# Triangular blocks of the DeltaNet inversion: substitution in blocks of sixteen, two per partition, merged to thirty-two on TensorE

## The chip, the core and the metric

The kernel runs on one core of a Trainium2 chip. The metric is the device time of one execution in microseconds (us); where several executions are timed, their median counts.

## What is computed

A trunk of two layers on a sequence of 1024 positions of width 1024. Each layer projects the normalised input once, gives the columns to three mixers (a convolution module, differential attention, and a gated DeltaNet in both directions), joins them in an output projection and ends in an MLP:

```python
u = rms_norm(x, pre_mix_w[l]) @ w_in[l]
y = concat([conv_module(u_conv, ...), diff_attention(dq, dk, dv, ...), gated_deltanet(gqkv, gz, ...)]) @ w_out[l]
x = x + rms_norm(y, post_mix_w[l])
x = x + rms_norm(square(relu(rms_norm(x, pre_mlp_w[l]) @ w_ff1[l])) @ w_ff2[l], post_mlp_w[l])
```

The change concerns the DeltaNet. It works in chunks of 64 positions, and each chunk, head (6) and direction (2) needs the solution with a unit lower triangular 64x64 matrix:

```python
A = where(strict, einsum("bhncd,bhnsd->bhncs", kb, kc) * decay, 0.0)
sol = triangular_solve(A, rhs, left_side=True, lower=True, unit_diagonal=True)
```

The scan over the 16 chunks (`step` in the reference) uses that solution, chunk after chunk.

## The kernel before

`w_in_phase` computes the input projection as dense items of 48 matmuls of 512 columns (L163 to L165, three products of high and low parts), in the order of the list `todo`: convolution inputs and DeltaNet q, k, v (`cp_0` to `cp_8`), attention q and k (`qkh`), attention v (`vt`), and the gate z (`zt`). Between the items two generators are advanced: `conv_module`, and `prep`, which makes for each of three head pairs p the masked products A (`dn_a`: transposes L652, squares `sq` on ACT L654, products of k and q L696, `R` and `De` on GpSimd L682 and L686, the powers `rkinv` and `rq` L670), and then runs `invert` for that pair beside `dn_a` of the next. The last five items of `todo` stand behind the end of `prep`; the DeltaNet scan (`scan`, first matmul L837) and its loads (`qkT`, `eg`, `vs`, `kta`) are advanced beside them.

`invert` (L736 to L804) turns the 64x64 triangles into their inverses. It writes A to DRAM (`ai`, L750) and reads it back so that each of the 128 partitions holds one diagonal block of 32x32 (`Lr`, `Lp`, L754); ACT transposes half of them (L755). On GpSimd, 31 rounds of two operations follow, each round a product with a column of `Lp` (L765, tile `subt`) and a subtraction in `Xm` (L766), on up to 256 elements per partition. ACT writes the transpose `XT` (L768). Both go to DRAM (`xi`, L770 and L771), and twelve loads bring them back as `Ta` and into the diagonal blocks of `Tt` (L779, L782). On TensorE, 64 products with `Ao` (the off-diagonal block of A) and 64 products with `Tt` give the off-diagonal block (L789 and L790, L797 and L798, tile Y between them on ACT); the inverse `Tt` is written to `kta` (L804). This runs six times, three pairs in two layers.

Every engine works through its own instructions in a fixed order, which a scheduler sets when the kernel is built: it lays the instructions out by a time plan of its own, so an edit in one function also moves instructions of others. Waits are by semaphores: an instruction that waits holds all that stands behind it on its engine. SP (SyncE) issues most of the DMAs, one after the other, in its order.

Of the kernel before, what the change touches and what calls it, by code (L numbers as in the profile page):

```python
# [9 lines left out]
F32 = mybir.dt.float32  # L10
F32R = mybir.dt.float32r
BF16 = mybir.dt.bfloat16
AF = mybir.ActivationFunctionType
ALU = mybir.AluOpType
# [4 lines left out]
P = 128  # L19
# [10 lines left out]
CH = 64  # L30
# [7 lines left out]
def make_consts():  # L38
    p = np.arange(P)
    t, s = p[:, None], p[None, :]  # L40
    same = (t // CH) == (s // CH)
    c64 = np.arange(CH)[None, :]
    pm = (p % CH)[:, None]
    cols, off = [], {}

    def add(name, a):
        a = np.asarray(a, np.float32)
        off[name] = (sum(c.shape[1] for c in cols), a.shape[1])
        cols.append(a)

    add("ident", np.eye(P))
    add("gt0", same & (t > s))
    add("gt1", same & (t < s))
    add("cum0", same & (t <= s))
    add("cum1", same & (t >= s))
    add("n0", np.where(pm <= c64, 30000.0, -30000.0))
    add("n1", np.where(pm >= c64, 30000.0, -30000.0))
    qs = np.zeros((P, 3))
    for j in range(3):
        for h in range(2):  # L60
            qs[64 * h:64 * h + 64, j] = -np.float32(DD ** -0.5) * 2.0 ** SLOPE_EXP[2 * j + h]
    add("qs", qs)
    return np.concatenate(cols, 1), off


CONSTS, COFF = make_consts()
BIAS = np.abs(np.arange(P)[:, None] - (np.arange(1920)[None, :] - 896)).astype(np.float16)

# [10 lines left out]
class K:  # L79
# [656 lines left out]
    def invert(self, l, p, A, X):  # L736

        nc = self.nc
        mm = nc.tensor.matmul
        nm = f"{l}_{p}"  # L740
        B = 32
        Lr = X.tile([P, B, B], F32, tag="Lr", bufs=2, name=f"Lr{nm}")
        Lp = X.tile([P, B, B], F32, tag="Lp", bufs=2, name=f"Lp{nm}")
        Af = [t.rearrange("p m h c -> p (m h) c") for t in A]
        Ao = X.tile([P, 16, B], F32, tag="Ao", bufs=1, name=f"Ao{nm}")
        for g in range(4):
            r = slice(g * B, (g + 1) * B)
            nc.sync.dma_start(Ao[r], Af[g % 2][r, :, B - (g % 2) * B:2 * B - (g % 2) * B])
        for d in range(2):
            nc.sync.dma_start(self.ai[p % 2][d], A[d].rearrange("p m h c -> p (m h c)"))  # L750
            dst = Lp if d else Lr
            for g in range(4):
                src = self.ai[p % 2][d, g * B:(g + 1) * B, :].rearrange("r (m c) -> m r c", c=CH)[:, :, (g % 2) * B:(g % 2 + 1) * B]
                nc.sync.dma_start(dst[64 * d + 16 * g:64 * d + 16 * g + 16], src)  # L754
        nc.scalar.activation(Lp[0:64], Lr[0:64].rearrange("p a b -> p b a"), AF.Copy)  # L755
        yield
        Xm = X.tile([P, B, B], F32, tag="Xm", bufs=1, name=f"Xm{nm}")
        XT = X.tile([P, B, B], F32, tag="Lr", bufs=2, name=f"XT{nm}")
        nc.gpsimd.memset(Xm, 0.0)
        nc.gpsimd.memset(Xm.rearrange("p a b -> p (a b)")[:, ::B + 1], 1.0)  # L760
        for j in range(B - 1):
            n, w = B - 1 - j, j + 1
            tmp = X.tile([P, 256], F32, tag="subt", bufs=1, name=f"subt{nm}_{j}")
            tv = tmp[:, 0:n * w].rearrange("p (a b) -> p a b", b=w)
            nc.gpsimd.tensor_tensor(tv, Lp[:, j + 1:, j:j + 1].broadcast_to([P, n, w]), Xm[:, j:j + 1, 0:w].broadcast_to([P, n, w]), op=ALU.mult)  # L765
            nc.gpsimd.tensor_tensor(Xm[:, j + 1:, 0:w], Xm[:, j + 1:, 0:w], tv, op=ALU.subtract)  # L766
            yield
        nc.scalar.activation(XT, Xm.rearrange("p a b -> p b a"), AF.Copy)  # L768
        xi = self.xi[p % 2]
        nc.sync.dma_start(xi[0], Xm)  # L770
        nc.sync.dma_start(xi[1], XT)  # L771
        Tt = [X.tile([P, NT, 2, CH], F32, tag=f"Tt{d}", bufs=1, name=f"Tt{nm}_{d}") for d in range(2)]
        for d in range(2):
            nc.gpsimd.memset(Tt[d], 0.0)
        Ta = X.tile([P, 16, B], F32, tag="iv", bufs=2, name=f"Ta{nm}")
        for g in range(4):
            r = slice(g * B, (g + 1) * B)
            for d in range(2):
                nc.sync.dma_start(Tt[d].rearrange("p m h c -> p (m h) c")[r, :, (g % 2) * B:(g % 2 + 1) * B],  # L779
                                  xi[1 - d, 64 * d + 16 * g:64 * d + 16 * g + 16].rearrange("m r c -> r m c"))  # L780
            d = g % 2
            nc.sync.dma_start(Ta[r], xi[d, 64 * d + 16 * g:64 * d + 16 * g + 16].rearrange("m r c -> r m c"))  # L782
        yield
        ps = self.dt_bank().rearrange("p (g c) -> p g c", c=B)
        Tf = [t.rearrange("p m h c -> p (m h) c") for t in Tt]
        for g in range(16):
            for hf in range(2):
                lo, hi = slice(64 * hf, 64 * hf + B), slice(64 * hf + B, 64 * hf + 2 * B)
                mm(ps[hi, g], lhsT=Ao[lo, g], rhs=Ta[lo, g], start=True, stop=True, tile_position=(64 * hf, 64 * hf + B))  # L789
                mm(ps[lo, g], lhsT=Ao[hi, g], rhs=Ta[hi, g], start=True, stop=True, tile_position=(64 * hf + B, 64 * hf))  # L790
        Y = X.tile([P, 16, B], F32, tag="iv", bufs=2, name=f"Y{nm}")
        nc.scalar.activation(Y, ps, AF.Copy, scale=-1.0)
        ps = self.dt_bank().rearrange("p (g c) -> p g c", c=B)
        for g in range(16):
            for hf in range(2):
                lo, hi = slice(64 * hf, 64 * hf + B), slice(64 * hf + B, 64 * hf + 2 * B)
                mm(ps[lo, g], lhsT=Y[hi, g], rhs=Tf[0][hi, g, B:], start=True, stop=True, tile_position=(64 * hf + B, 64 * hf))  # L797
                mm(ps[hi, g], lhsT=Y[lo, g], rhs=Tf[1][lo, g, :B], start=True, stop=True, tile_position=(64 * hf, 64 * hf + B))  # L798
        for hf in range(2):
            lo, hi = slice(64 * hf, 64 * hf + B), slice(64 * hf + B, 64 * hf + 2 * B)  # L800
            nc.scalar.activation(Tf[0][lo, :, B:], ps[lo], AF.Copy)
            nc.vector.tensor_copy(Tf[1][hi, :, :B], ps[hi])
        for d in range(2):
            nc.sync.dma_start(self.kta[d, :, :, 1, p].rearrange("m q c -> q m c"), Tt[d].rearrange("p m h c -> p m (h c)"))  # L804
# [800 lines left out]
```

## Time and profile before

| | before |
|---|---|
| runs | 2982.74, 2984.09, 2980.22 us, median 2982.74 |
| profiled execution | 2982.14 us, of it span 2980.3 us |
| mean granted TensorE clock | 0.955 |
| PE (TensorE) busy | 2726.6 us, 91% |
| DVE (VectorE) busy | 2093.7 us, 70% |
| ACT (ScalarE) busy | 1391.1 us, 47% |
| POOL (GpSimd) busy | 892.1 us, 30% |
| chain that ended last | PE 65%, POOL 11%, DVE 8%, DMA 8% |

Busy time says how long an engine had work in progress; the chain that ended last follows the work back from the last instruction, at each step to what it waited for. The clock column of the windows is the share of full speed (2.4 GHz; the lower level is 1.2 GHz, shown as 0.5) that was granted. A number in brackets behind a row of the timeline is the time that the engine stood idle before it, and what released it.

### The profile page before, as it was taken

Reading aid. Unit: us, or ns where it says so; the run is one execution under the profiler, and the core shown is the slowest. Engines: PE = TensorE matmul, PEld = TensorE weight load, DVE = VectorE, ACT = ScalarE, POOL = GpSimd, SP = SyncE. Lnnn points to the kernel's source line nnn. Section 1 sums busy time; section 2 is a strip of 40 time slices with the busy share of each in tenths; the row PEclk is TensorE's granted clock in tenths of the full one; section 3 lists DMA queues with packets and bytes.
Section 4 is the critical chain, followed back from the end, with each engine's and each line's share of the span. In section 5 each row is a group of like instructions: output and inputs, shape, how many; then the busy total and the mean of one; then the engine's idle time right before and its main releaser. Section 6 shows DMA issues by size and latency. Waiting matters only on the chain.

```text
span 2980.3 us, 46140 instructions
## 1 busy us (share of the span) xinstructions
PE 2726.6 (91%) x17292; PEld 2184.5 (73%) x17292; DVE 2093.7 (70%) x3717; ACT 1391.1 (47%) x2436; POOL 892.1 (30%) x801
## 2 busy tenths in 40 slices
PE   8977979988999998999799689799989999989996
PEld 7865757766888886888687567577668888878885
DVE  5796327888487776777757772279874877767776
ACT  5432326676256664333354223266863566643232
POOL 2288716756000000000313986267541000000002
PEclk9998979999999999999899889799989999999998
DMA  5557785433235558664446486844332355586643
GB/s 136 152 153 210 207 201 154 120 102 124 81 110 212 200 196 315 224 213 165 130 121 140 130 244 188 213 133 124 101 120 85 114 211 201 216 335 223 215 142 113
DMA packets 415313, 504.74 MB, mean 169 GB/s; under 512 B 125401, under 2 KB 313945, under 8 KB 412786
## 3 DMA queue, kind: packets, MB, share of 16 engines
q1 hardware_dynamic: 359362, 373.92, 42.0%
q10 hardware_dynamic: 55728, 127.88, 11.2%
q8 instruction: 136, 2.23, 0.3%
q14 instruction: 87, 0.71, 0.1%
HBM read 318.01 MB, written 182.12 MB: 168 GB/s over the span
## 4 chain that ended last, share of the span: by engine, by line
PE 65%; POOL 11%; DVE 8%; DMA 8%; issue 4%; ACT 2%; SPq 2%; ACTq 0%; DVEq 0%; POOLq 0%
PE at L163 10%; PE at L164 10%; PE at L165 10%; POOL Xm L766 4%; PE sc L163 4%; PE sc L164 4%; PE sc L165 4%; POOL subt L765 3%; PE at L1044 2%; PE dt L163 2%; PE dt L165 2%; PE dt L164 2%; PE tr L1070 2%; DVE sc L1046 2%; PE tr L1079 2%
## 5 line engine op out<-in xcount | busy, mean ns | idle before, releaser
L246 POOL TENSOR_TENSOR y<-y,mgP 128x1024 f32<-128x1024 f32 x8 | 21.8, 2737 | 1247.5 <-ACT jk L242 1247.5
L163 PE MATMUL at<-hTh,wh 128*128 128x512 f32 (+1 forms) x832 | 328.1, 396 | 7.7 <-ACT cp L363 7.7
L165 PE MATMUL at<-hTh,wl 128*128 128x512 f32 (+1 forms) x832 | 326.7, 394 | 6.9 <-DVE wl L169 6.9
L164 PE MATMUL at<-hTl,wh 128*128 128x512 f32 (+1 forms) x832 | 327.5, 394 | 0.0
L1049 ACT ACTIVATE sc<-sc,mx 128x1024 f32<-128x1024 f32 x192 | 220.8, 1152 | 88.8 <-DVE mx L1046 88.6
L163 PEld LDWEIGHTS at<-hTh,wh 128*128 128x128 f32 x832 | 161.3, 194 | 39.6 <-ACT cp L363 8.5
L165 PEld LDWEIGHTS at<-hTh,wl 128*128 128x128 f32 x832 | 160.9, 194 | 39.5 <-DVE wl L169 8.4
L164 PEld LDWEIGHTS at<-hTl,wh 128*128 128x128 f32 x832 | 161.6, 194 | 31.2 <-issue 0.8
L491 DVE SCALAR_TENSOR_TENSOR ca<-cu,dw,ca 128x1024 f32<-128x1024 f32 x120 | 170.6, 1437 | 0.4
L1044 PE MATMUL at<-stk 96*128 96x512 f32 x352 | 144.9, 470 | 16.1 <-DVE mx L1046 14.9
L1046 DVE CUSTOM_DVE_ANT_0 sc<-at,bias,mx 128x512 f32<-128x512 f32 x192 | 142.3, 745 | 21.8 <-PE at L1044 16.3
L1046 DVE CUSTOM_DVE_ANT_0 sc<-at,bias 128x512 f32<-128x512 f32 x192 | 130.0, 684 | 35.4 <-PE at L1044 32.1
L1156 ACT ACTIVATE ob<-sb 128x512 fp32r<-128x512 f32 x120 | 74.2, 626 | 171.8 <-PE tr L165 45.4
L765 POOL TENSOR_TENSOR subt<-Lp,Xm 128x31 f32<-128x31 f32 (+15 forms) x186 | 129.5, 696 | 82.9 <-DMA Lp<-ai 25.8
L766 POOL TENSOR_TENSOR Xm<-Xm,subt 128x31 f32<-128x31 f32 (+15 forms) x186 | 144.3, 776 | 13.0
L163 PE MATMUL at<-ob,oa 128*128 128x512 f32 x356 | 138.5, 391 | 1.0 <-DVE y L1482 1.0
L164 PE MATMUL at<-ob,oa 128*128 128x512 f32 x356 | 139.0, 391 | 0.0
L165 PE MATMUL at<-ob,oa 128*128 128x512 f32 x356 | 138.9, 390 | 0.0
L1156 ACT ACTIVATE ob<-w2r 128x512 fp32r<-128x512 f32 x92 | 57.3, 627 | 141.7 <-PE tr L165 52.2
L1070 PE MATMUL tr<-consts,sc 128*128 128x128 f32 x704 | 108.0, 284 | 12.9 <-DVE sc L1066 6.0
L169 DVE TENSOR_TENSOR wl<-wr,wh 128x1024 fp32r<-128x1024 f32 x48 | 65.1, 1356 | 72.4 <-ACT wh L168 72.4
L1157 DVE TENSOR_TENSOR ob<-sb,ob 128x512 fp32r<-128x512 f32 x120 | 81.6, 686 | 41.3 <-ACT ob L1156 41.3
(459 smaller groups left out, 7950.7 us busy)
## 6 DMA issues: line engine op xcount, KB each, us to landing
hd<-oa ACTq DMA_DIRECT2D x120, 512.0 KB, 5.8
oa<-hd SPq DMA_DIRECT2D x120, 512.0 KB, 4.3
w1r<-in_w_ff_dram SPq DMA_DIRECT2D x32, 1024.0 KB, 5.6
w2r<-in_w_ff_dram SPq DMA_DIRECT2D x64, 512.0 KB, 6.5
wr<-in_w_in_dram SPq DMA_DIRECT2D x50, 512.0 KB, 5.2
ld<-hd SPq DMA_DIRECT2D x98, 256.0 KB, 3.9
kta<-kta SPq DMA_DIRECT2D x32, 576.0 KB, 9.4
stk<-qk SPq DMA_DIRECT2D x66, 256.0 KB, 6.2
```

The costliest lines, as they stand in the source:

```text
L163: mm(ps, lhsT=lh, rhs=rh, start=first, stop=False, skip_group_check=more)
L164: mm(ps, lhsT=lh, rhs=rl, start=False, stop=False, skip_group_check=more)
L165: mm(ps, lhsT=ll, rhs=rh, start=False, stop=last, skip_group_check=more)
L491: nc.vector.scalar_tensor_tensor(ca, u[:, k:k + S], dw[:, i, k:k + 1], ca, ALU.mult, ALU.add)
L765: nc.gpsimd.tensor_tensor(tv, Lp[:, j + 1:, j:j + 1].broadcast_to([P, n, w]), Xm[:, j:j + 1, 0:w].broadcast_to([P, n, w]), op=ALU.mult)
L766: nc.gpsimd.tensor_tensor(Xm[:, j + 1:, 0:w], Xm[:, j + 1:, 0:w], tv, op=ALU.subtract)
L1044: mm(ps, lhsT=st[:, 0, t * P:(t + 1) * P], rhs=st[:, 1, ks], start=True, stop=True)
L1046: nc.vector.tensor_tensor_reduce(out=sc[:, ks], in0=ps, in1=self.bias[:, o:o + 512], scale=slope, scalar=mx[:, 0:1] if n2 else 3.0e38, op0 ...
L1049: nc.scalar.activation(sc, sc, AF.Exp, scale=-1.0, bias=mx[:, 1:2], accum_out=oS[:, t, mp:mp + 1])
L1070: nc.tensor.transpose(ps[:, k], pp[0][:, (4 * q + k) * P:(4 * q + k + 1) * P], self.ident)
L1156: self.nc.scalar.activation(h, src, AF.Copy)
L1157: self.nc.vector.tensor_tensor(lo, src, h.bitcast(F32), op=ALU.subtract)
```

## The change

Substitution is done in blocks of sixteen. Each partition still holds its 32x32 block, but GpSimd works on the two 16x16 blocks of the diagonal at once: 15 rounds of two operations on up to 128 elements. `Lp` has one buffer instead of two, `subt` two instead of one. What joins the two halves of a block of 32 is new: tiles `Oz` (two per inversion) hold the off-diagonal 16x16 blocks, set to zero by GpSimd and filled by ACT with row masks `rm0` and `rm1`; a tile `Tb` holds the other orientation of the inverse; sixteen loads of `xi` take the place of twelve. TensorE then makes 128 products of 32 columns with `Oz` (ACT copies the result back into `Oz`), 64 for `Ta`, and 128 of 64 columns for `Tt`, and VectorE subtracts the results from `Ta` and `Tt`. The step to 64 is as before. All 32x32 work of TensorE keeps its four diagonal positions.

```diff
@@ -60,6 +60,8 @@
         for h in range(2):
             qs[64 * h:64 * h + 64, j] = -np.float32(DD ** -0.5) * 2.0 ** SLOPE_EXP[2 * j + h]
     add("qs", qs)
+    add("rm0", (p % 32 < 16)[:, None])
+    add("rm1", (p % 32 >= 16)[:, None])
     return np.concatenate(cols, 1), off
 
 
@@ -738,9 +740,18 @@
         nc = self.nc
         mm = nc.tensor.matmul
         nm = f"{l}_{p}"
-        B = 32
-        Lr = X.tile([P, B, B], F32, tag="Lr", bufs=2, name=f"Lr{nm}")
-        Lp = X.tile([P, B, B], F32, tag="Lp", bufs=2, name=f"Lp{nm}")
+        B, H = 32, 16
+        W = H * B + H
+
+        def blocks(t):
+
+            return t.rearrange("p (x k) -> p x k", k=W)[:, :, 0:H * B].rearrange("p x (a b) -> p x a b", b=B)
+
+        def square(t):
+            return t[:, 0:B * B].rearrange("p (a b) -> p a b", b=B)
+
+        Lr = X.tile([P, 2 * W], F32, tag="Lr", bufs=2, name=f"Lr{nm}")
+        Lp = X.tile([P, 2 * W], F32, tag="Lp", bufs=1, name=f"Lp{nm}")
         Af = [t.rearrange("p m h c -> p (m h) c") for t in A]
         Ao = X.tile([P, 16, B], F32, tag="Ao", bufs=1, name=f"Ao{nm}")
         for g in range(4):
@@ -748,41 +759,80 @@
             nc.sync.dma_start(Ao[r], Af[g % 2][r, :, B - (g % 2) * B:2 * B - (g % 2) * B])
         for d in range(2):
             nc.sync.dma_start(self.ai[p % 2][d], A[d].rearrange("p m h c -> p (m h c)"))
-            dst = Lp if d else Lr
+            dst = square(Lp if d else Lr)
             for g in range(4):
                 src = self.ai[p % 2][d, g * B:(g + 1) * B, :].rearrange("r (m c) -> m r c", c=CH)[:, :, (g % 2) * B:(g % 2 + 1) * B]
                 nc.sync.dma_start(dst[64 * d + 16 * g:64 * d + 16 * g + 16], src)
-        nc.scalar.activation(Lp[0:64], Lr[0:64].rearrange("p a b -> p b a"), AF.Copy)
+
+        Oz = [X.tile([P, 16, B], F32, tag="Oz", bufs=2, name=f"Oz{nm}_{d}") for d in range(2)]
+        for d in range(2):
+            nc.gpsimd.memset(Oz[d], 0.0)
+            o = H - H * d
+            for g in range(4):
+                r = slice(g * B, (g + 1) * B)
+                nc.scalar.activation(Oz[d][r, :, o:o + H], Af[d][r, :, (g % 2) * B + o:(g % 2) * B + o + H], AF.Copy, scale=self.C[f"rm{d}"][r])
+        nc.scalar.activation(square(Lp)[0:64], square(Lr)[0:64].rearrange("p a b -> p b a"), AF.Copy)
         yield
-        Xm = X.tile([P, B, B], F32, tag="Xm", bufs=1, name=f"Xm{nm}")
-        XT = X.tile([P, B, B], F32, tag="Lr", bufs=2, name=f"XT{nm}")
+        Xm = X.tile([P, 2 * W], F32, tag="Xm", bufs=1, name=f"Xm{nm}")
+        XT = X.tile([P, 2 * W], F32, tag="Lr", bufs=2, name=f"XT{nm}")
         nc.gpsimd.memset(Xm, 0.0)
-        nc.gpsimd.memset(Xm.rearrange("p a b -> p (a b)")[:, ::B + 1], 1.0)
-        for j in range(B - 1):
-            n, w = B - 1 - j, j + 1
-            tmp = X.tile([P, 256], F32, tag="subt", bufs=1, name=f"subt{nm}_{j}")
-            tv = tmp[:, 0:n * w].rearrange("p (a b) -> p a b", b=w)
-            nc.gpsimd.tensor_tensor(tv, Lp[:, j + 1:, j:j + 1].broadcast_to([P, n, w]), Xm[:, j:j + 1, 0:w].broadcast_to([P, n, w]), op=ALU.mult)
-            nc.gpsimd.tensor_tensor(Xm[:, j + 1:, 0:w], Xm[:, j + 1:, 0:w], tv, op=ALU.subtract)
+        nc.gpsimd.memset(Xm[:, 0:B * B:B + 1], 1.0)
+        Lb, Xb = blocks(Lp), blocks(Xm)
+        for j in range(H - 1):
+            n, w = H - 1 - j, j + 1
+            tmp = X.tile([P, 128], F32, tag="subt", bufs=2, name=f"subt{nm}_{j}")
+            tv = tmp[:, 0:2 * n * w].rearrange("p (x a b) -> p x a b", x=2, b=w)
+            nc.gpsimd.tensor_tensor(tv, Lb[:, :, j + 1:, j:j + 1].broadcast_to([P, 2, n, w]), Xb[:, :, j:j + 1, 0:w].broadcast_to([P, 2, n, w]), op=ALU.mult)
+            nc.gpsimd.tensor_tensor(Xb[:, :, j + 1:, 0:w], Xb[:, :, j + 1:, 0:w], tv, op=ALU.subtract)
             yield
-        nc.scalar.activation(XT, Xm.rearrange("p a b -> p b a"), AF.Copy)
+        nc.scalar.activation(square(XT), square(Xm).rearrange("p a b -> p b a"), AF.Copy)
         xi = self.xi[p % 2]
-        nc.sync.dma_start(xi[0], Xm)
-        nc.sync.dma_start(xi[1], XT)
+        nc.sync.dma_start(xi[0], square(Xm))
+        nc.sync.dma_start(xi[1], square(XT))
         Tt = [X.tile([P, NT, 2, CH], F32, tag=f"Tt{d}", bufs=1, name=f"Tt{nm}_{d}") for d in range(2)]
         for d in range(2):
             nc.gpsimd.memset(Tt[d], 0.0)
+
         Ta = X.tile([P, 16, B], F32, tag="iv", bufs=2, name=f"Ta{nm}")
+        Tb = X.tile([P, 16, B], F32, tag="ivb", bufs=1, name=f"Tb{nm}")
+        for g in range(4):
+            r = slice(g * B, (g + 1) * B)
+            for d in range(2):
+                nc.sync.dma_start((Tb if d != g % 2 else Ta)[r], xi[d, 64 * d + 16 * g:64 * d + 16 * g + 16].rearrange("m r c -> r m c"))
         for g in range(4):
             r = slice(g * B, (g + 1) * B)
             for d in range(2):
                 nc.sync.dma_start(Tt[d].rearrange("p m h c -> p (m h) c")[r, :, (g % 2) * B:(g % 2 + 1) * B],
                                   xi[1 - d, 64 * d + 16 * g:64 * d + 16 * g + 16].rearrange("m r c -> r m c"))
-            d = g % 2
-            nc.sync.dma_start(Ta[r], xi[d, 64 * d + 16 * g:64 * d + 16 * g + 16].rearrange("m r c -> r m c"))
         yield
+        Tf = [t.rearrange("p m h c -> p (m h) c") for t in Tt]
+        V = []
+        for d in range(2):
+            ps = self.rot_bank().rearrange("p (g c) -> p g c", c=B)
+            for m in range(16):
+                for g in range(4):
+                    r = slice(g * B, (g + 1) * B)
+                    mm(ps[r, m], lhsT=Oz[d][r, m], rhs=(Tb if d != g % 2 else Ta)[r, m], start=True, stop=True, tile_position=(g * B, g * B))
+            V.append(Oz[d])
+            nc.scalar.activation(V[d], ps, AF.Copy)
+
+        pa = self.rot_bank().rearrange("p (g c) -> p g c", c=B)
+        for m in range(16):
+            for g in range(4):
+                r = slice(g * B, (g + 1) * B)
+                mm(pa[r, m], lhsT=Tf[g % 2][r, m, (g % 2) * B:(g % 2 + 1) * B], rhs=V[g % 2][r, m], start=True, stop=True, tile_position=(g * B, g * B))
+        nc.vector.tensor_tensor(Ta, Ta, pa, op=ALU.subtract)
+        yield
+        for mg in range(2):
+            for d in range(2):
+                ps = self.rot_bank().rearrange("p (g c) -> p g c", c=CH)
+                for m in range(8):
+                    for g in range(4):
+                        r = slice(g * B, (g + 1) * B)
+                        mm(ps[r, m], lhsT=V[d][r, 8 * mg + m], rhs=Tf[d][r, 8 * mg + m], start=True, stop=True, tile_position=(g * B, g * B))
+                sl = slice(8 * mg, 8 * mg + 8)
+                nc.vector.tensor_tensor(Tf[d][:, sl], Tf[d][:, sl], ps, op=ALU.subtract)
         ps = self.dt_bank().rearrange("p (g c) -> p g c", c=B)
-        Tf = [t.rearrange("p m h c -> p (m h) c") for t in Tt]
         for g in range(16):
             for hf in range(2):
                 lo, hi = slice(64 * hf, 64 * hf + B), slice(64 * hf + B, 64 * hf + 2 * B)
```

The new order of instructions, as built. On TensorE in layer 0, the first product of inversion 0; `at` is a bank of a dense item, `sc` and `dt` banks of the inversion. Before, the second half of `dn_a` of pair 2 (L696) and then dense work stood there, and the first product of inversion 0 came later:

```order
850 L163 MATMUL at_2826<-hTh_92,wh_2821 128x512
851 L164 MATMUL at_2826<-hTl_93,wh_2821 128x512
852 L165 MATMUL at_2826<-hTh_92,wl_2822 128x512
853 L696 MATMUL tr_2028<-kq_2_1835 64x128 x7
854 L696 MATMUL tr_2029<-kq_2_1835 64x128 x7
...
907 L165 MATMUL at_2897<-hTh_92,wl_2893 128x512
908 L163 MATMUL at_2897<-hTh_92,wh_2892 128x512
909 L789 MATMUL dt_1563<-Ta_0_1550,Ao_0_1092 32x32
```

Now, with the line numbers of the changed kernel (L815 is the product with `Oz`, L698 what was L696):

```order
787 L166 MATMUL at_3101<-hTl_93,wh_3070 128x512
788 L167 MATMUL at_3101<-hTh_92,wl_3071 128x512
789 L815 MATMUL sc_1405<-Ta_0_1387,Oz_0_0_1107 32x32
790 L815 MATMUL sc_1405<-Tb_0_1388,Oz_0_0_1107 32x32
791 L815 MATMUL sc_1405<-Ta_0_1387,Oz_0_0_1107 32x32
...
1147 L848 MATMUL dt_1810<-Tt_0_1_1384,Y_0_1808 32x32
1148 L698 MATMUL tr_2798<-kq_2_2653 64x128
1149 L698 MATMUL tr_2799<-kq_2_2653 64x128
```

The products of inversion 0 now stand ahead of the second half of `dn_a` of pair 2, and inside `cp_8` (bank `at_3101`), one dense item and more before their old place.

On TensorE at the end of that stage, the first step of the scan (`vs` times `kta`), before:

```order
1802 L164 MATMUL at_4105<-hTl_93,wh_4074 128x512
1803 L165 MATMUL at_4105<-hTh_92,wl_4075 128x512
1804 L837 MATMUL sc_3427<-vs_0_3409,kta_0_3410 64x64 x2
1805 L837 MATMUL sc_3428<-vs_0_3409,kta_0_3410 64x64 x2
1806 L837 MATMUL sc_3427<-vs_0_3409,kta_0_3410 64x64 x6
```

and now:

```order
2344 L167 MATMUL at_4794<-hTh_92,wl_4790 128x512
2345 L165 MATMUL at_4794<-hTh_92,wh_4789 128x512
2346 L887 MATMUL sc_4336<-vs_0_4318,kta_0_4319 64x64 x2
2347 L887 MATMUL sc_4337<-vs_0_4318,kta_0_4319 64x64 x2
2348 L166 MATMUL at_4794<-hTl_93,wh_4789 128x512
2349 L167 MATMUL at_4794<-hTh_92,wl_4790 128x512
```

It stood behind the last dense matmul, and now stands between dense matmuls, with more of them behind it.

On ACT in layer 0, the transposes `XT` and the squares `sq` of pair 2, before:

```order
145 L372 ACTIVATE cacc_7_2343<-cacc_7_2343 128x1024
146 L654 ACTIVATE sq_2_1_0_1881<-tr_1876 128x512
147 L373 DMA gq<-cacc_7_2343 128x1024
148 L768 ACTIVATE XT_0_1109<-Xm_0_1108 128x1024
149 L654 ACTIVATE sq_2_1_1_1895<-tr_1890 128x512
```

and now:

```order
144 L774 ACTIVATE Lp_1_1930<-Lr_1_1929 64x1024
145 L773 ACTIVATE Oz_1_0_1946<-A_1_0_1200,consts 32x16x16 x4
146 L656 ACTIVATE sq_2_0_0_2663<-tr_2658 128x512
147 L773 ACTIVATE Oz_1_1_1947<-A_1_1_1201,consts 32x16x16 x4
...
152 L842 ACTIVATE Y_0_1808<-dt_1743 128x512
153 L656 ACTIVATE sq_2_1_0_2681<-tr_2676 128x512
154 L788 ACTIVATE XT_1_1960<-Xm_1_1959 128x1024
155 L656 ACTIVATE sq_2_1_1_2689<-tr_2684 128x512
```

The last `sq` of pair 2 stood behind `XT` of inversion 0 and now stands behind `XT` of inversion 1, and the first `sq` stands behind the copies into `Oz` of inversion 1.

## Rows read from the trace of the kernel before

**Rows 1.** The page: busy times of TensorE, and the two groups of the substitution.

```profile
PE 2726.6 (91%) x17292; PEld 2184.5 (73%) x17292; DVE 2093.7 (70%) x3717; ACT 1391.1 (47%) x2436; POOL 892.1 (30%) x801
...
L765 POOL TENSOR_TENSOR subt<-Lp,Xm 128x31 f32<-128x31 f32 (+15 forms) x186 | 129.5, 696 | 82.9 <-DMA Lp<-ai 25.8
L766 POOL TENSOR_TENSOR Xm<-Xm,subt 128x31 f32<-128x31 f32 (+15 forms) x186 | 144.3, 776 | 13.0
```

**Rows 2.** Windows: length, busy of PE, PEld, DVE, ACT, POOL, clock, DMA.

```profile
150.00:200.00 50.00, 41.69 (x193) 33.20 (x186) 43.87 (x50) 17.70 (x20) 42.78 (x37) 0.90 0.50 124
...
395.00:440.00 45.00, 28.86 (x236) 21.77 (x234) 8.64 (x25) 8.37 (x17) 13.61 (x12) 0.58 0.93 223
...
1880.00:1920.00 40.00, 19.56 (x194) 15.34 (x195) 6.32 (x18) 6.36 (x12) 13.61 (x12) 0.62 0.95 227
```

**Rows 3.** Waits of TensorE, 150 to 440 us: total, times, longest.

```profile
PE tr L696 <- ACT sq L654: 19.4, 2, 18.0
PE sc L837 <- DMA kta<-kta: 10.3, 2, 5.4
PE at L1044 <- DMA stkE<-qk: 5.0, 1, 5.0
...
PE tr L620 <- DVE Aqk L701: 3.4, 2, 3.2
```

**Rows 4.** The same for layer 1, 1630 to 1920 us.

```profile
PE tr L696 <- ACT sq L654: 16.8, 1, 16.8
PE sc L837 <- DMA kta<-kta: 10.6, 2, 5.9
PE at L1044 <- DMA stkE<-qk: 8.9, 1, 8.9
PE tr L620 <- DVE Aqk L701: 6.6, 1, 6.6
```

**Rows 5.** Timeline of TensorE, layer 0: start, duration, then idle before.

```profile
197.12 0.39 PE L165 MATMUL at<-hTh,wl 128*128 128x512 f32 x1
...
236.51 1.97 PE L696 MATMUL tr<-kq 64*64 64x128 f32 x18 [18.01 <-ACT sq L654]
...
239.43 0.63 PE L165 MATMUL at<-hTh,wl 128*128 128x512 f32 x1
```

**Rows 6.** Timelines of ACT, SP and TensorE behind the end of inversion 0.

```profile
234.04 1.94 ACT L768 ACTIVATE XT<-Xm 128x1024 f32<-128x1024 f32 x1 [16.67 <-POOL Xm L766]
...
234.03 0.33 SPq L770 DMA_DIRECT2D xi<-Xm  x1
...
249.20 0.49 SPq L782 DMA_DIRECT2D Ta<-xi  x1
...
251.53 0.24 PE L789 MATMUL dt<-Ta,Ao 32*32 32x32 f32 x2
```

**Rows 7.** Timeline of SP at the end of the stage, layer 0.

```profile
390.51 1.16 SPq L719 DMA_DIRECT2D qkT<-gq  x1
```

**Rows 8.** Timeline of GpSimd, inversion 2 of layer 0, and TensorE's first product.

```profile
323.05 0.25 POOL L765 TENSOR_TENSOR subt<-Lp,Xm 128x31 f32<-128x31 f32 x1 [6.19 <-ACT Lp L755]
...
325.34 0.38 POOL L765 TENSOR_TENSOR subt<-Lp,Xm 128x112 f32<-128x112 f32 x1
...
343.80 0.73 POOL L766 TENSOR_TENSOR Xm<-Xm,subt 128x256 f32<-128x256 f32 x1
...
366.15 0.25 POOL L766 TENSOR_TENSOR Xm<-Xm,subt 128x31 f32<-128x31 f32 x1
...
378.98 0.21 PE L790 MATMUL dt<-Ta,Ao 32*32 32x32 f32 x1 [0.60 <-DMA Ta<-xi]
```

**Rows 9.** Timeline of GpSimd, inversion 0 of layer 0.

```profile
155.81 1.40 POOL L765 TENSOR_TENSOR subt<-Lp,Xm 128x31 f32<-128x31 f32 x1 [25.85 <-DMA Lp<-ai]
...
197.33 2.03 POOL L686 TENSOR_TENSOR De<-De,rho 128x512 f32<-128x512 f32 x1
...
202.85 0.69 POOL L766 TENSOR_TENSOR Xm<-Xm,subt 128x255 f32<-128x255 f32 x1
...
233.76 0.25 POOL L766 TENSOR_TENSOR Xm<-Xm,subt 128x31 f32<-128x31 f32 x1
```

**Rows 10.** Timeline of TensorE: first and last of 64 products of 32 columns.

```profile
263.71 0.21 PE L797 MATMUL dt<-Tt,Y 32*32 32x32 f32 x1
...
264.97 0.19 PE L798 MATMUL dt<-Tt,Y 32*32 32x32 f32 x1
```

**Rows 11.** Layer 1: a dense matmul of TensorE, and the thirtieth operation of inversion 0.

```profile
1655.16 0.39 PE L165 MATMUL at<-hTh,wl 128*128 128x512 f32 x1
...
1681.69 1.54 POOL L766 TENSOR_TENSOR Xm<-Xm,subt 128x255 f32<-128x255 f32 x1
```

## The prediction

> **What bounds the kernel now.** I read the page first: TensorE is busy for 2726.6 us, 91% of the span, and the substitution (L765 and L766, 62 operations per inversion, six inversions) costs GpSimd 273.8 us in all [rows 1]. The reader should see two things: TensorE is nearly full, so work added to it is paid somewhere; and GpSimd's 274 us are no gain in themselves, because only the time in which TensorE stands still can be won. So I looked for that idle time, stage by stage. In the stage of the input projection the windows show where it lies: the granted clock is 0.58 in 395 to 440 us of layer 0 and 0.62 in 1880 to 1920 us of layer 1, with TensorE busy for 28.86 of 45 and 19.56 of 40 us [rows 2]. The waits of TensorE name the causes, per layer: one long wait for ACT's `sq` (18.0 and 16.8 us), two waits for DeltaNet's `kta` loads (10.3 and 10.6 us together) and one for `stkE` (5.0 and 8.9 us) [rows 3, 4]. In the timeline, TensorE stops after 218 us in the middle of `dn_a` of pair 2 and resumes at 236.51 [rows 5]: ACT's `sq` stands in its queue behind `XT`, which waited 16.67 us for the last `Xm` of inversion 0 [rows 6]. So the chain on GpSimd reaches TensorE through one queue position on ACT, once per layer, and a second time at the end, where the `kta` and DeltaNet loads start only once inversion 2 is written (SP issues them from 390.51 us) [rows 7].
>
> **What the change removes.** (a) The chain itself. Undisturbed, an operation of 112 elements takes 0.38 us and one of 256 elements 0.73 us, with gaps of some 0.08 us [rows 8]; thirty operations of at most 128 elements are then about 13 us, where inversion 2 of layer 0 took 43 (323.05 to 366.40 [rows 8]). Beside a busy VectorE (43.87 of 50 us [rows 2]) the same operation takes about 1.5 us whatever its size: 1.40 us for 31 elements [rows 9] against 0.25 where nothing disturbs [rows 8]. The first thirty operations of inversion 0 end at 203.5 us in before, counting from 155.81, with GpSimd's `R`, `De` and powers between them. From that I take off 4.4 us for the smaller tiles (1240 elements fewer, twice, at 0.0018 us an element from the two rows above) and part of two `De` steps that now come behind the chain (2.03 us each [rows 9]). So Xm of inversion 0 ends near 197 us instead of 234.0, and that of layer 1 near 1677 (worked out below).
> (b) The 18.0 and 16.8 us waits in their present form, and some 2 us of half-speed work behind each (the dense matmul at 239.43 takes 0.63 us where it takes 0.39 at full clock [rows 5]): −20 and −19 us.
> (c) The end of the stage. In the new order the first scan steps stand inside the dense items `zt_1` and `zt_2` (second order excerpt), since inversion 2 is done some 40 us earlier against the dense work. If so, the waits for `kta` and `stkE` are covered by dense matmuls: 10.3 + 5.0 = 15.3 us in layer 0, 19.5 in layer 1. The clock follows: of the 28.86 us busy at 0.58 some 12 are slowness, of the 19.56 at 0.62 some 7.4. That makes −27 us for each layer.
> (d) Small idle times in 270 to 345 and 1740 to 1775 us, among them waits of 3.2 and 6.6 us for DVE's `Aqk` [rows 3, 4], that lie beside other waits of the new order: −7 and −9.5.
>
> **What it adds on TensorE.** 192 products of 32 columns and 128 of 64 columns per inversion. 64 products of 32 columns run in 1.26 us, from 263.71 to 264.97 [rows 10], so 20 ns each; the first kind is 3.8 us. For 64 columns no row exists: the ends are 20 ns (the same) and 40 ns (twice the columns), 2.6 to 5.1 us; I take 3.4, nearer to the short end, as the row beside it holds a start and a drain as well. Together 7.2 us per inversion, 22 us per layer, 43 in all (range 38 to 54). None of it is hidden, as TensorE is the engine that the stage waits on.
> The Trainium skill, page TensorEngine Tiling (Array Packing), section Instruction Overhead, says that a matmul costs about 60 cycles however few its columns are. At 25 ns each, an estimate from that page, the 320 products would be 8.0 us an inversion and 48 in all; our row of 20 ns shows the four quadrants overlapping better than that, and 5 us would not turn the sign.
>
> **What it moves: new waits of TensorE.** This decides. TensorE works in a fixed order, and the new order puts the products of the merge early (first order excerpt): in layer 0 `Oz_0` stands after only 30 dense matmuls of `cp_8`, which TensorE reaches at 197.12 us [rows 5]. The data are not there. From the end of Xm to TensorE's first matmul on the loaded `Ta` it took 17.5 us in before: xi was issued at 234.03, the last `Ta` load at 249.20 (SP needs 10 us for twelve loads), and the matmul came at 251.53 [rows 6]. Now there are sixteen loads, `Ta` and `Tb` first, so the first product can come at 197 + 16 = 213 us: a hole of about 15.5 us. It is the old 18 us wait at another place.
> Then, walking along the new order with rows of before for each step: about 10 us where `sq` of pair 2 stands behind the new `Oz_1` copies on ACT, which need GpSimd's memset that itself follows four rounds of inversion 1 (third excerpt); 4.5 us where the last `sq` again stands behind `XT_1`, since inversion 1 starts near 229 us (SP must issue the sixteen loads, `ai_1` and eight `Lr`/`Lp` loads before, and the ACT transpose follows) and ends near 250; 6 us at `Oz_1`, which comes only some 24 us of work after `Oz_0`; 6 us for the loads of `Tt_1`, whose memset waits for the write of `Tt_0`; 3 us at `Oz_2`. Sum: 45 us in layer 0 (bounds 10 and 75: none but half of the first, or all of them 60% longer).
> In layer 1 the place of `Oz_0` is even earlier, in `cp_7`: the dense matmul before it starts at 1655.16 us in before, 1665 with the small waits around it, and Xm ends near 1677: the thirtieth operation at 1681.69 + 1.54 [rows 11] less the same 4.4 and the `De` steps. With the 17.5 us that gives 1694 and a hole of 29 us. The others as in layer 0: 57 us (bounds 20 and 85).
> The other additions cost nothing that shows: five VectorE subtractions and two ACT copies of some 0.7 us per inversion lie between products that wait for each other (their latency is in the walk above), the ACT copies into `Oz` replace no one on the path, and GpSimd's two small memsets stand in a chain that is already counted to 197 us.
>
> **Sum.** Layer 0: −20 −27 −7 + 22 + 45 = +13. Layer 1: −19 −27 −9.5 + 22 + 57 = +23.5. Together +36.5 us on the profiled execution of 2982.14 us, which lies 0.6 us below the median of the three runs, so 2982.7 + 36 = 3019.
>
> **Rivals.**
> A, faster: the data come ahead of TensorE. Where DMA queues were quiet (inversion 2, 366.40 to 378.98 [rows 8]) the loads took 12.6 us, not 17.5, and without VectorE beside it the chain takes 13 us, not 40. If half of that holds, the hole at `Oz_0` falls to some 3 us in layer 0 and 15 in layer 1, and the later ones halve: holes of 18 and 30 us. Layer 0: −54 + 22 + 18 = −14; layer 1: −55.5 + 22 + 30 = −3.5; with all small holes gone another −15. That gives 2945 to 2970. For it: GpSimd is the only one whose work shrinks, and less of it disturbs VectorE. Against it: inversions 0 and 1 ran through the busy windows in before, and their operations will again.
> B, no change: the covered end of the stage (54 us) pays the added products (43 us) and the moved waits equal the old ones: 2977 to 2988.
> C, slower by far: the chain counts operations, not elements. If nearly all thirty operations of inversions 0 fall beside VectorE at 1.5 us plus a gap, thirty take 47 us instead of the 25 that are left for them in the walk, and everything on TensorE after `Oz_0` comes 15 to 20 us later in each layer: 3019 + 35 = 3054. It decides from the point at which more than two of three operations are disturbed; in the first thirty of before it was under half. The Trainium skill, page GPSIMD Engine Reference, section Key points, says that GpSimd shares its SBUF interfaces with VectorE and contends with instructions of two inputs there; by that rule the length of the chain goes by VectorE's work, and the rows on the 31-element operation agree (1.40 against some 0.25 us).
> D, the change does not do what it says: if the chain still set the end of the stage, the waits for `kta` would stay and the time would be 3019 + 45. The new order speaks against it, and I fold it into C.
>
> **How the numbers follow.** Forecast (2989 to 3035) 0.45; A 0.32; B 0.10; C with D 0.13. The likeliest gives 3019. The range must leave out 2 in 10 at most: it goes from 2940, past the middle of A, to 3056, past C's price. About 0.2%, 6 us, is what a measurement of this kernel can tell from no change; faster by more than that 0.32, within it 0.10, slower 0.58.
>
> **What would show it.** L765 with 90 operations and below 70 us in all; the wait of TensorE for `sq` at L696 down, and in its place waits at the `Oz` products for `Ta` or `Tb`, about 15 us in layer 0 near 197 us and 29 in layer 1 near 1665; no wait for `kta` at the first scan step; the granted clock near full at the old end of the stage; TensorE's busy time up by 30 to 45 us. The prediction is wrong if the waits at `Oz` are under 5 us each (A), or if time moves in attention, the output projection or the MLP, whose order the scheduler also rewrote and which I cost at nothing.

## The result

The changed kernel takes 3065.44 us (median of 4, 3055.26 to 3081.54) against 2983.41 us before: ratio 1.0277, 95% interval 1.0240 to 1.0315. It is slower, as forecast, but by 82 us where 36 were forecast, and beyond the upper end of the range (3056). The profiled execution of the changed kernel took 3055.26 us, its span 3053.5; that is the fastest of its runs, and the spans of the two traces differ by 73.2 us.

The page of the changed kernel: busy time per engine, then the row of TensorE's program loads (queue 8, "instruction"), then the two groups of the substitution from the view of GpSimd's groups.

```profile
PE 2785.7 (91%) x21132; PEld 2238.7 (73%) x21132; DVE 2094.5 (69%) x3747; ACT 1425.7 (47%) x2496; POOL 721.3 (24%) x621
...
q8 instruction: 167, 2.74, 0.4%
...
L785 POOL TENSOR_TENSOR subt<-Lp,Xm 128x30 f32<-128x30 f32 (+7 forms) x90 | 53.2, 591 | 127.7 <-DMA Lp<-ai 96.7 <-ACT Lp L774 25.2
L786 POOL TENSOR_TENSOR Xm<-Xm,subt 128x30 f32<-128x30 f32 (+7 forms) x90 | 51.1, 568 | 6.4
```

Against [rows 1] the substitution fell from 273.8 to 104.3 us, and TensorE's busy time rose by 59.1 us. The loads of TensorE's program rose from 136 packets, 2.23 MB, to 167, 2.74 MB.

The waits of TensorE in 150 to 440 us, which answer to [rows 3]: total, times, longest.

```profile
PE sc L815 <- DMA Ta<-xi: 11.1, 3, 6.9
PE tr L654 <- ACT Kt L659: 7.7, 1, 7.7
PE sc L832 <- issue: 7.1, 4, 2.6
PE sc L823 <- issue: 4.5, 1, 4.5
PE dt L815 <- issue: 4.2, 1, 4.2
PE dt L832 <- issue: 3.3, 2, 1.9
...
PE dt L823 <- issue: 3.2, 1, 3.2
...
PE dt L840 <- issue: 2.9, 1, 2.9
```

The 18 us wait for `sq`, the `kta` and the `stkE` waits are gone, in layer 1 too. In their place stand short waits for `Ta`, and a kind that hardly existed before: idle time that ends with nothing that the profile shows ("issue"), always at or just behind the small products L815, L823, L832. Over the whole span the rows of this kind add up to 3.1 us in before and 47.1 us here; all other waits of TensorE together fell from 220.2 to 189.4 us.

The time is lost where the forecast looked for it. The first transpose of layer 1 (L227, now L229) comes 33.6 us late (1480.67 against 1514.31 us), the last product of layer 1's attention 75.5 us late (2208.9 against 2284.4), and the span ends 73.2 us later: outside the two stages of the input projection next to nothing is lost.

The windows that answer to [rows 2], layer 0:

```profile
200.00:230.00 30.00, 18.88 (x659) 16.68 (x660) 27.39 (x35) 7.20 (x7) 2.90 (x4) 0.54 0.85 204
395.00:440.00 45.00, 45.00 (x223) 36.66 (x222) 10.26 (x24) 11.12 (x20) 8.00 (x8) 1.00 0.67 185
```

The old end of the stage is now full at full clock, as forecast. The low clock has moved to the merge of inversion 0, 0.54 in 200 to 230 us.

Here is one merge in the timeline of TensorE (start, duration, idle before): four places in inversion 0, one in inversion 1, and a stretch of inversion 2.

```profile
202.06 0.28 PE L815 MATMUL sc<-Ta,Oz 32*32 32x32 f32 x2 [6.86 <-DMA Ta<-xi]
...
213.11 0.74 PE L832 MATMUL sc<-Tt,Oz 32*32 32x64 f32 x18 [2.14 <-issue]
218.58 0.47 PE L823 MATMUL dt<-Oz,Tt 32*32 32x32 f32 x18 [3.23 <-issue]
...
224.47 1.96 PE L832 MATMUL sc<-Tt,Oz 32*32 32x64 f32 x64
...
266.93 0.26 PE L815 MATMUL dt<-Ta,Oz 32*32 32x32 f32 x1 [4.16 <-issue]
...
367.48 1.08 PE L832 MATMUL dt<-Tt,Oz 32*32 32x64 f32 x64
```

Each product leaves two matmul records, so 64 records are 32 products: 34 ns a product at full clock (1.08 us), 61 ns at half (1.96 us). The merge of inversion 0 runs from 202 to 226 us, 24 us, with the waits and a few dense matmuls between, for what I had priced at 7.2.

What ends the "issue" idles is seen in the view of the DMA queues, cut to 0.1 us at 264.1 us, in the middle of the 4.16 us idle (the share is that of these 0.1 us):

```profile
q8 instruction: 1, 0.02, 84.9%
```

A load of TensorE's program, 16384 bytes, starts there, and TensorE goes on 2.8 us later. It is so at each of the eight "issue" idles of over 1 us up to 300 us: loads start at 210.57, 216.38, 220.46, 264.13, 276.33, 281.92, 286.59 and 294.20 us, and TensorE resumes 2.2 to 2.9 us behind each (213.11, 218.58, 223.40, 266.93, 278.70, 284.17, 289.00, 296.45). The ten later ones of this trace, in both layers, end the same way.

### The profile page after: what moved, and what is told of

Same layout as the page of the kernel before. It is cut to its first block, busy times and chain, and to the rows that moved or that the text cites. A ratio compares the mean times of both kernels' runs of the same rounds, so it can differ in the third digit from the quotient of the medians.

```text
span 3053.5 us, 53771 instructions
## 1 busy us (share of the span) xinstructions
PE 2785.7 (91%) x21132; PEld 2238.7 (73%) x21132; DVE 2094.5 (69%) x3747; ACT 1425.7 (47%) x2496; POOL 721.3 (24%) x621
## 3 DMA queue, kind: packets, MB, share of 16 engines
q8 instruction: 167, 2.74, 0.4%
## 4 chain that ended last, share of the span: by engine, by line
PE 70%; DVE 9%; DMA 7%; POOL 5%; issue 4%; SPq 2%; ACT 2%; DVEq 0%; ACTq 0%; POOLq 0%
PE at L165 11%; PE at L166 11%; PE at L167 11%; PE sc L165 4%; PE sc L166 4%; PE sc L167 4%; DVE sc L1096 2%; PE at L1094 2%; PE dt L166 2%; PE dt L165 2%; PE dt L167 2%; PE dt L911 2%; POOL subt L785 2%; PE dt L909 2%; POOL Xm L786 2%
## 5 line engine op out<-in xcount | busy, mean ns | idle before, releaser
L1099 ACT ACTIVATE sc<-sc,mx 128x1024 f32<-128x1024 f32 x192 | 220.2, 1148 | 60.9 <-DVE mx L1096 53.0
L493 DVE SCALAR_TENSOR_TENSOR ca<-cu,dw,ca 128x1024 f32<-128x1024 f32 x120 | 160.8, 1360 | 0.4
L166 PE MATMUL at<-ob,oa 128*128 128x512 f32 x352 | 137.0, 389 | 0.0
L167 PE MATMUL at<-ob,oa 128*128 128x512 f32 x352 | 136.5, 389 | 0.0
L165 PE MATMUL at<-ob,oa 128*128 128x512 f32 x352 | 136.0, 389 | 0.0
L1114 POOL TENSOR_TENSOR sc<-sc,sc 128x1024 f32<-128x1024 f32 x40 | 104.1, 2606 | 30.6 <-ACT sc L1111 29.8
L1124 ACT ACTIVATE aT<-tr 128x512 f32<-128x512 f32 x160 | 92.0, 593 | 30.0 <-PE tr L1120 29.7
```

The lines of the kernel that those rows point to most:

```text
L165: mm(ps, lhsT=lh, rhs=rh, start=first, stop=False, skip_group_check=more)
L166: mm(ps, lhsT=lh, rhs=rl, start=False, stop=False, skip_group_check=more)
L167: mm(ps, lhsT=ll, rhs=rh, start=False, stop=last, skip_group_check=more)
L493: nc.vector.scalar_tensor_tensor(ca, u[:, k:k + S], dw[:, i, k:k + 1], ca, ALU.mult, ALU.add)
L1099: nc.scalar.activation(sc, sc, AF.Exp, scale=-1.0, bias=mx[:, 1:2], accum_out=oS[:, t, mp:mp + 1])
L1114: self.lastpool = nc.gpsimd.tensor_tensor(pp[0], pp[0], pp[1], op=ALU.add)
```

## The theories

The 3840 matmul records more come with as many weight loads; 7680 records over 31 more loads of the program are 248 per load. So one load holds about 64 products of four records each, which run in 1.3 us [rows 10], and no two loads in this trace start closer than 3.4 us. **Theory L**: rows of small products use up TensorE's program faster than it is loaded; TensorE waits for the load, falls to the lower clock, and runs the next products at half pace. **Rival E**: the products cost their engine time, the rest is moved waits. **Rival W**: order and waits for the loads of `Ta` and `Tt` decide. A second pair asks what a shorter chain is worth, in the kernel before. **Q**: the place of `sq` behind `XT` in ACT's queue is what costs. **C**: the end of the stage waits for the chains on GpSimd and what follows them.

## Experiments

Ratios are to the kernel before in the same session, where it took 2983 to 2988 us.

**The products of 64 columns left out**, and their subtraction:

```diff
-        for mg in range(2):
-            for d in range(2):
-                ... 32 products of 64 columns ...
-                nc.vector.tensor_tensor(Tf[d][:, sl], Tf[d][:, sl], ps, op=ALU.subtract)
```

> The changed kernel without the 128 products of 64 columns per inversion and their four subtractions (so the triangles are not merged to thirty-two in Tt); everything else stays. Theory L (loading): TensorE's program is loaded in blocks of 256 instructions, one small product is four, and a row of small products runs at the pace of the loads, about 4 us for 64 products, instead of 1.3 us. Then 128 products cost two blocks, about 8 us an inversion, 48 in all: 3065 falls to about 3017, and waits of TensorE without a releaser in the trace fall with it. Rival E (engine time): a product costs its 20 to 27 ns, the rest of the loss are the moved waits: 3065 falls by about 20 to 3045. Rival W (waits): the order and the waits for loads decide: within 10 us of 3065.

Measured 2993.54 us (ratio 1.0030, 1.0018 to 1.0042): 72 us less than the change. "Issue" waits fell from 47.1 to 11.7 us. By the two traces, 59.9 us apart, 35.4 us of it are "issue" time and 25.5 us busy time. E, which had 20, and W are out; L has the sign and the waits, but 72 is half again its 48. 768 products cost 94 ns each.

**The same products twice:**

```diff
-                        mm(ps[r, m], lhsT=V[d][r, 8 * mg + m], rhs=Tf[d][r, 8 * mg + m], start=True, stop=True, tile_position=(g * B, g * B))
+                        for _ in range(2):
+                            mm(ps[r, m], lhsT=V[d][r, 8 * mg + m], rhs=Tf[d][r, 8 * mg + m], start=True, stop=True, tile_position=(g * B, g * B))
```

> The changed kernel with each of the 128 products of 64 columns issued twice, the second over the first; the result is unchanged. L: plus two blocks per inversion, about 8 us, 48 in all: 3113. E: plus 3.4 us per inversion, 20 in all: 3085. W: within 10 us of 3065.

Measured 3120.08 us (ratio 1.0467, 1.0443 to 1.0491), 55 us more: L's size. But the "issue" waits are 49.5 us, only 2.4 more; TensorE's busy time rose by 41.4 us, 54 ns for each product more, and the waits for ACT by 15. So the doubled products are paid mostly as engine time, not as idle time: at 34 ns each they would be 26 us, and the mean granted clock is 0.944 against 0.953. L had the size here and not the mechanism. An estimate from the rows above fits: 64 products at the 61 ns of half clock take 3.9 us, longer than the 3.4 us between two loads, so at that clock the loads need not hold them up. No run tests this by itself.

**The kernel before with 320 idle products per inversion, and with the same engine time in wide matmuls:**

```diff
+        for k in range(3):
+            pd = self.rot_bank().rearrange("p (g c) -> p g c", c=B)
+            for m in range(16):
+                for g in range(4):
+                    r = slice(g * B, (g + 1) * B)
+                    mm(pd[r, m], lhsT=Ta[r, m], rhs=Ta[r, m], ...)
+        for mg in range(2):
+            for d in range(2):
+                ... 32 products lhsT=Ta[r, 8 * mg + m], rhs=Tf[d][r, 8 * mg + m] ...
```

```diff
+        for k in range(5):
+            pd = self.rot_bank()
+            ... 8 products of Ta, 32 columns ...
+            for m in range(6):
+                mm(pd, lhsT=hTh[:, 0, 0:P], rhs=hTh[:, 0, 0:512], start=True, stop=True)
```

> The kernel before with 320 products more per inversion, of the sizes of the change, on the loaded Ta and Tt ahead of Y; nothing reads their results, the substitution stays in blocks of thirty-two. L: five blocks at about 4 us, 20 us per inversion, 120 in all less what falls into idle time: 3065 to 3100. E: 7.2 us per inversion, 43 in all: 3026. W: the products fall mostly into time in which TensorE waits anyway: under 3005.

> The kernel before with the same engine time in few instructions: per inversion 30 matmuls of 512 columns (0.227 us each, 6.8 us) and 40 small products (0.8 us), behind the same loads; nothing reads their results. 220 instructions instead of 1280. L: only the engine time, 7.6 us per inversion, 46 in all: about 3028, that is 40 to 70 us less than with the 320 products. E: the same as with the 320 products, within 10 us. W: under 3005.

Measured 3140.61 us (ratio 1.0526, 1.0500 to 1.0552) with the products and 3078.39 us (1.0322, 1.0301 to 1.0343) with the wide matmuls. The waits of TensorE without a releaser, first with the products (the largest rows), then with the wide matmuls (all):

```profile
PE sc L790 <- issue: 24.1, 8, 5.4
PE dt L790 <- issue: 14.8, 4, 4.7
PE tr L652 <- issue: 7.9, 3, 4.4
```

```profile
PE tr L652 <- issue: 6.8, 3, 4.4
```

The difference of 62 us lies where L put it, and it is the "issue" time: 65.4 against 6.8 us over all rows. E, which had both alike, falls, and so does W. Not all "issue" time is loading: the waits at L652 are in both runs, and no load of TensorE's program starts in the 16 us before the longer ones. And L was too low in size: 3140.61 lies above its 3100, and the wide ones cost 93 us, twice the 46 that L gave for their time alone (E 43). Most of the wide matmuls (161 of 180) start at full clock, like the first six:

```profile
256.72 1.65 PE L793 MATMUL sc<-hTh 128*128 128x512 f32 x6
```

What comes on top lies around them. TensorE's waits grew by 25.1 us in all (223.3 to 248.4), with new ones for `Ta` (longest 22.3 us) and `kta` in the new order, and of its busy time 197.9 us passed at half clock, where it was 150.7 before: 47 us more, of which about half are lost. Added work behind these loads was paid about twice even without program loads.

**The change without its merge** (blocks of sixteen alone; the off-diagonal sixteens stay out of the result):

```diff
-        Oz = [X.tile([P, 16, B], F32, tag="Oz", bufs=2, name=f"Oz{nm}_{d}") for d in range(2)]
-        ... memset and masked copies into Oz, Tb and its loads ...
-        ... all 320 products, copies to V, subtractions ...
```

> The changed kernel without what joins the blocks of sixteen: no Oz, no Tb, none of the 320 products, no copies and subtractions (the off-diagonal blocks of sixteen stay out of the result); fifteen rounds, twelve loads. It is the shorter chain alone. Theory L (the loss of the change is the loading of TensorE's program in rows of small products, beside their engine time): nothing of it is left, and the gain of the shorter chain shows: the waits for sq (18 and 17 us) shrink and the kta loads come early: 2915 to 2960, below the kernel before. Rival W (the moved waits cost most): the early place of the first products and the loads remain, 2985 to 3030.

Measured 2948.25 us (ratio 0.9867, 0.9848 to 0.9886), within L's range. The shorter chain alone is worth 38 us, and what joins the halves costs 117 us (3065.44 against 2948.25), its loads and copies and the order that comes with them included. In the traces the span grows by 108.8 us from this kernel to the changed one: TensorE busy 55.3 (2730.4 to 2785.7), "issue" waits 40.1 (7.0 to 47.1), waits for DMAs 25.6 (49.7 to 75.3), less 12 in the other waits.

**XT on GpSimd in the kernel before, and then xi written from GpSimd's queue too:**

```diff
-        nc.scalar.activation(XT, Xm.rearrange("p a b -> p b a"), AF.Copy)
+        nc.gpsimd.tensor_copy(XT, Xm.rearrange("p a b -> p b a"))
```

```diff
-        nc.sync.dma_start(xi[0], Xm)
-        nc.sync.dma_start(xi[1], XT)
+        nc.gpsimd.dma_start(xi[0], Xm)
+        nc.gpsimd.dma_start(xi[1], XT)
```

> The kernel before with XT made by GpSimd instead of ACT, so that sq on ACT no longer stands behind the end of the chain; all else stays, blocks of thirty-two. Theory Q (the queue position on ACT costs its wait): minus 18 and 17 us and the half clock behind, 2983 falls to about 2945. Rival C (the end of the stage waits for the chain on GpSimd and what follows it, so the time won in the middle is waited for at the end): the wait at sq is gone, the waits for kta at the end of the stage grow by as much, 2975 to 2990.

> As the one with XT on GpSimd, and the two writes of xi issued from GpSimd's queue instead of SP's, so that SP does not stand at the end of each chain and loads the next block ahead of it. Q: as there, 2945. C: chains 1 and 2 begin 8 to 10 us earlier each, the end of the stage by 16 to 20 us per layer: 2983 falls to 2940 to 2955; the loads of Ta come no later than before.

The first took 2980.16 us (ratio 0.9981, 0.9966 to 0.9996). Its waits of TensorE, layer 0:

```profile
PE dt L789 <- DMA Ta<-xi: 14.7, 1, 14.7
PE sc L837 <- DMA kta<-kta: 9.6, 2, 5.2
PE at L1044 <- DMA stkE<-qk: 5.8, 1, 5.8
```

The wait at `sq` is down to 2.3 us, and TensorE stands 14.7 us at the first product instead: the hole belongs to the chain and its loads, not to ACT's queue. Q falls. C has the time but not the place: the waits for `kta` did not grow (9.6 us against 10.3). The second took 3001.74 us (ratio 1.0051, 1.0032 to 1.0071), which neither had. Its second and third chains began only 1.3 and 1.9 us earlier (244.29 and 321.11 us in the trace), and the wait for `kta` grew to 16.4 us. What made these loads late I did not settle.

**The third inversion on VectorE, blocks of thirty-two; then XT as well; then the second inversion too:**

```diff
+            eng = nc.vector if p == 2 else nc.gpsimd
-            nc.gpsimd.tensor_tensor(tv, ...)
-            nc.gpsimd.tensor_tensor(Xm[:, j + 1:, 0:w], ...)
+            eng.tensor_tensor(tv, ...)
+            eng.tensor_tensor(Xm[:, j + 1:, 0:w], ...)
```

> The kernel before, blocks of thirty-two, with the 62 operations of the third inversion of each layer on VectorE instead of GpSimd; nothing else. VectorE is busy for 24 of 95 us there, and its row of 128x256 elements takes 0.4 us where GpSimd's takes 0.65 to 0.73. Theory C (the end of the stage waits for the chains on GpSimd and what follows them): the third chain takes 22 to 28 us instead of 43, and the stage ends 15 to 20 us earlier in each layer: 2985 falls to 2945 to 2955. Rival Q (only the hole at sq counts): no change, 2980 to 2990.

> As the one before it, and XT of the first two inversions on GpSimd instead of ACT. C: the end no longer hides what the hole at sq costs, so the 18 and 17 us count too, in part (the first products still wait for Ta some 15 us): 2930 to 2945. Q: 2980, as with XT on GpSimd alone.

> The kernel before with the second and the third inversion of each layer on VectorE (62 operations each); the first stays on GpSimd. C: the second chain, 67 us on GpSimd, takes some 35 to 45 us on VectorE, the third begins by as much earlier, and the end of the stage stops waiting for it: 2966, as with the third alone, falls to 2935 to 2955. Rival V (VectorE, 70 of 100 us busy in the second chain's time, becomes the bound there): its other work comes 20 us later, 2965 to 2990.

The third alone: 2965.61 us (ratio 0.9928, 0.9910 to 0.9945), less than both kernels. The last operation of that chain, and TensorE's longest waits in 150 to 440 us:

```profile
354.21 0.19 DVE L767 TENSOR_TENSOR Xm<-Xm,subt 128x31 f32<-128x31 f32 x1
```

```profile
PE tr L696 <- ACT sq L654: 19.3, 2, 18.0
PE sc L838 <- DMA kta<-kta: 4.3, 1, 4.3
PE at L1045 <- DMA stkE<-qk: 4.0, 1, 4.0
```

The chain ends at 354.4 us instead of 366.4, and one of the two `kta` waits is gone, though the hole at `sq` still stands at its 18.0 us. That is C's mechanism, though a smaller gain than C gave. With XT on GpSimd as well it is 2967.84 us (ratio 0.9931, 0.9908 to 0.9954): no more gain, so C was wrong that the hole would now count; TensorE waits 12.0 us for `Ta` instead. With the second inversion on VectorE too it is 2985.06 us (ratio 0.9989, 0.9975 to 1.0003): V. There the second chain takes 76 us among VectorE's other work (245.5 to 321.1 us), longer than the 67 us on GpSimd, and the wait for `kta` grows to 24.7 us.

## Why the prediction was wrong

**The chain** was right: inversion 0 of layer 0 ends at 194.6 us (forecast 197), inversion 1 runs from 226.9 to 247.4 (229 to 250). L765's successor has 90 operations and 53.2 us. Two slips in the working did not matter: the slope of the two rows is 0.0024 us an element, not 0.0018 (0.35 us over 144 elements), so the 4.4 us should have been 6; and the waits of layer 1 add up to 58.5 us, not 57.

**The end of the stage** was right: no wait for `kta`, clock 1.00 in 395 to 440 us.

**The new waits** were over-sized. The first `Ta` and `Tb` loads were landed and used 7.4 us after the chain, at 202.06 us, not 16: the order puts them first, and SP issued the first at 197.66 us. I had taken the time to the last of twelve loads of before as the time to the first of sixteen. The hole at `Oz_0` is 6.9 us, not 15.5, in layer 1 11.8, not 29; the wait behind the new `Oz` copies is 7.7 and 10.5 us (forecast 10), at ACT's `Kt`, which stands behind them.

**The failed step is the price of the products**: 7.2 us per inversion, 43 in all, as engine time and nothing else. By the two traces TensorE's busy time rose by 59.1 us (forecast 30 to 45) and its "issue" time by 44.0: 103 us where 43 were priced. The 128 products of 64 columns alone, 20 us in the forecast, are worth 72 us when they are left out.

The term that was put at nothing is the load of the program, these 44 us. The 64 products of [rows 10] could not show it: they are about one load, and stand alone between dense matmuls that start 0.23 us apart. The rest is smaller. At full clock the products would be 49 us, an estimate from 1152 at 20 ns [rows 10] and 768 at 34 ns (the row at 367.48, which lies within my bounds of 20 to 40). And 175.0 us of TensorE's busy time passed at half clock, against 150.7 before: about half of the 24 us more is lost. Six in ten of the new products' records begin at that clock, behind the "issue" waits or behind a wait for `Ta`, and a product of 64 columns then takes 61 ns.

**The sum** came out nearer than its terms, which is luck: the products were under-sized by 60 us, and the rest over-sized by 24, for the other waits fell by 30.8 us where the rest of the forecast gave −7 (36.5 less 43). My upper bound took the worst of the waits, and for the products only a wider row, not another mechanism; that is why 3065 lay outside. Rival C of the prediction gave about the right time (3054) for a reason that did not occur: of the first inversion's thirty operations 9 took over 1 us.

## What to carry to other kernels

On TensorE, price a stage of many tiny matmuls by its instruction count as well as by its columns: look for idle time that nothing releases, and whether a program load lies in it. A stage measured alone between long matmuls says little of five such stages in a row. And when a wait on one queue is long, move what it really waits for (here the chain on GpSimd, by putting the third inversion on VectorE, which had time there), not the instruction that happens to stand behind it.

## What the runs showed of the hardware

TensorE's program is loaded in blocks of 16384 bytes during the run, not closer than 3.3 us apart in these traces (3.4 with the change), each start followed by TensorE's resuming 2.2 to 2.9 us later where it had run dry. The Trainium skill, page Runtime: NRT & Kernel Launch, section Instruction fetch mechanics, says that the program is streamed in blocks of 16 KiB (256 instructions) and that crossing a block is mostly hidden. The block size agrees with the 248 records per load here. "Mostly hidden" holds for the kernel before (3.1 us of such waits) and not for rows of small products (47.1 us with the change, 65.4 us with the idle products in the kernel before, of which 7.9 us at L652 are no loading).

What sets the 3.3 us between loads the runs do not show. Nor do they separate how much of the low clock comes from these waits and how much from the waits for data around them: at inversion 0 the granted clock was 0.50 in 202 to 206 us, behind 6.86 us of waiting for `Ta` and ahead of the first "issue" wait.
